# Stationary-weight units: order of high and low parts, and the columns at which their tiles start

## Chip, cores, metric

The kernel runs on one core of a Trainium2 chip. The metric is the device time of one execution in microseconds (us).

## What is computed

One decoder layer on 256 tokens of width 2048, in float32: a combined input projection, two token mixers (gated linear attention and forgetting attention), a merge and an output projection, a LayerNorm, a gated MLP of width 5632 with a causal convolution, a LayerNorm, and a gated embedding. Cut to the products that matter here:

```
proj = x @ w_in                        # gq, gk, gv, gr, glr, fq, fk, fv, ff, ma, mb
...
def conv_gated_mlp(x, w_gate, w_up, conv_w, conv_b, w_down):
    g = causal_dwconv(x @ w_gate, conv_w, conv_b)
    h = jax.nn.gelu(g) * (x @ w_up)
    return h @ w_down
```

The columns fq, fk (1024 each), gq, gk (1024 each) and the two matrices w_gate and w_up (5632 columns each) are the ones whose products the change touches.

## The kernel before

TensorE multiplies in the type float32r, which keeps fewer bits than float32. So each float32 operand is kept as two tiles, a high part (the value rounded to float32r) and a low part (what is left), and a product is three: high by high, high by low, low by high.

All weights come as units of 128 x 2048 floats, numbered 0 to 283 in the order of their use. `prep` loads a unit on SP's queue in two halves of 1024 columns (`raw`), makes the high part of each half on ScalarE (`hi`, by `copy`) and the low part on VectorE (`lo`, raw minus high). The tiles `hi` come from the pool `rhi`, the tiles `lo` from `rlo`, six buffers each. `unit()` hands out the next unit and prepares up to three ahead. TensorE and the other compute engines run in the order that a scheduler writes at build time; SP's queue runs in program order.

There are two ways to use a unit on TensorE:

- Stationary weights (`w_unit`): a unit holds 16 blocks of 128 rows by 128 output columns. For each block the high part is the stationary operand and the activation tile (x high and x low side by side, 512 columns) moves past it; then the low part is stationary and x high (256 columns) moves past. All 32 matmuls add into one bank of PSUM. This is done for fq and fk (units 0 to 15, `psfq`, `psfk`, with activations `xT`), for gq and gk (16 to 31, `psq`, `psk`) and for w_gate and w_up in turn (136 to 223, even numbers `psg`, odd `psu`, with activations `x1T`). The first three units of the last group go token half by token half through `w_phase` instead, with 256 columns in each matmul; so `w_unit` serves 117 units.
- Stationary activations (`q_unit`, `s_half`, `x_half`; lines 979, 841 and 353): the activation is stationary and 512 columns of `hi` or `lo` move. All other units go this way.

Small matmuls of other work are pulled in between: `tick(7)` in `w_unit` pulls one step of the attention after the eighth low matmul of a unit.

The tiles lie in SBUF one behind the other, and a pool's buffers lie at steps of the tile's width. Counted in float32 columns, `xT` and `x1T` start at a multiple of 64, and so do the buffers of `rhi` (1024 wide) and of `rlo` (1152 wide). `lo_tile` takes 1024 of the 1152 columns, from column 16 on in the stationary-weight units and from column 0 on in all others (`UA`, `LO_SHIFT`). "Place" below means a tile's first column within a period of 64. Some other tiles happen to lie at place 48: the stationary activation sums `xS` of two pairs (line 841), and the values `vh`, `vl` that move at line 1084.

Of the kernel before, what the change touches and what calls it, by code (L numbers as in the profile page):

```python
# [10 lines left out]
F32R = mybir.dt.float32r  # L11
# [8 lines left out]
P = 128  # L20
# [15 lines left out]
GAPS = (96, 64, 80)  # L36


LO_SHIFT = 16
UA = (range(32, 136), range(224, 284))  # L40
P_STAT = 5000
P_LN1 = (4000, 2000)
P_LN2 = (4000, 1000)
# [35 lines left out]
def tile_block(ctx: ExitStack, tc: tile.TileContext, wu, wfv, wpp, xT_in, x_in, pT_in, wlr,  # L79
               chan, gnorm, lng, ident_in, mask_in, cmask_in, out):  # L80
    nc = tc.nc
# [9 lines left out]
    rhi = ctx.enter_context(tc.tile_pool(name="rhi", bufs=6))  # L91
    rlo = ctx.enter_context(tc.tile_pool(name="rlo", bufs=6))
# [12 lines left out]
    def s8(shape, dt=F32, name=None):  # L105
        return big.tile(shape, dt, tag="S8", name=name)

    def t1(name):
        return sm.tile([P, 256], F32, tag="t1", bufs=6, name=name)
# [4 lines left out]
    def mmtile(name):  # L114
        return pmm.tile([P, 512], F32, tag="mm", name=name)
# [4 lines left out]
    def copy(o, i, scale=1.0):  # L120
        return nc.scalar.activation(o, i, AF.Copy, bias=0.0, scale=scale)  # L121
# [12 lines left out]
    n_prep, n_used = [0], [0]  # L134
# [15 lines left out]
    sd = dr.tile([len(DN_S[0]) // 2, P, 2048], F32, name="sd")  # L150
    hS = {}

    def lo_tile(u, name):
        o = 0 if any(u in r for r in UA) else LO_SHIFT
        return rlo.tile([P, 1152], F32R, tag="lo", name=f"lo{name}")[:, o:o + 1024]

    def differences(r0, r1, h, pinned=False):
        b12, b11, b22, b21 = r0[:, 0:512], r0[:, 512:1024], r1[:, 0:512], r1[:, 512:1024]
        sub = lambda o, a, b: nc.vector.tensor_tensor(o, a, b, ALU.subtract)  # L159
        if h == 0:  # L160
            i = sub(b11, b12, b11)
            if pinned:
                tc.keep_in_program_order(i)
            sub(b12, b12, b22)
        else:
            sub(b22, b22, b11)
            sub(b21, b21, b22)
# [17 lines left out]
    def prep_s(u):  # L185


        r0, r1 = [ring.tile([P, 1024], F32, tag="raw", bufs=5, name=f"raw{u}_{h}")
                  for h in range(2)]
        b12, b11, b22, b21 = r0[:, 0:512], r0[:, 512:1024], r1[:, 0:512], r1[:, 512:1024]  # L190
        rt = (r0, r1)
        if u in parked:
            nc.sync.dma_start(b11, wu[u, :, 512:1024])
            nc.sync.dma_start(r1, wu[u, :, 1024:2048])
            w = s8([P, 2048], name=f"td{u}")
            nc.sync.dma_start(w, td[parked[u]])
            rt = (w[:, 0:1024], w[:, 1024:2048])
        else:
            for h, r in enumerate((r0, r1)):
                nc.sync.dma_start(r, wu[u, :, h * 1024:(h + 1) * 1024])  # L200
        if dn0 <= u < dn0 + NF:
            nh = (u - dn0) // (NF // 2)
            pair = DN_ORDER[nh][(u - dn0) % (NF // 2)]
            i = DN_S[0].index(pair)
            if i % 2 == 0:
                two = s8([P, 8, 256], F32R, name=f"hS{nh}_{pair}")
                nc.sync.dma_start(two.bitcast(F32), sd[i // 2].rearrange(
                    "p (i n) -> p i n", i=8))
                hS[nh, pair], hS[nh, DN_S[0][i + 1]] = two[:, 0:4], two[:, 4:8]

        def split(src, name, e=slice(0, 1024)):
            hi = rhi.tile([P, 1024], F32R, tag="hi", name=f"hi{u}_{name}")[:, e]
            lo = lo_tile(u, f"{u}_{name}")[:, e]
            copy(hi, src)
            nc.vector.tensor_tensor(lo, src, hi.bitcast(F32), ALU.subtract)  # L215
            return [(hi[:, o:o + 512], lo[:, o:o + 512]) for o in range(0, src.shape[1], 512)]

        x11, = split(b11, "b11", slice(512, 1024))
        x22, x21 = split(r1, "b2")
        if u not in parked:  # L220
            differences(r0, r1, 0)
        t3, t1_ = split(rt[0], "t13")
        if u not in parked:
            differences(r0, r1, 1)
        t2_, t4 = split(rt[1], "t24")
        ready[u] = [x11, x21, x22, t1_, t3, t2_, t4]

    def prep(pinned=False):
        u = n_prep[0]
        n_prep[0] += 1  # L230
        if u in s_units:
            prep_s(u)
            return
        his, los = [], []
        for h in range(2):
            raw = ring.tile([P, 1024], F32, tag="raw", bufs=5, name=f"raw{u}_{h}")
            nc.sync.dma_start(raw, wu[u, :, h * 1024:(h + 1) * 1024])
            hi = rhi.tile([P, 1024], F32R, tag="hi", name=f"hi{u}_{h}")
            copy(hi, raw)
            lo = lo_tile(u, f"{u}_{h}")  # L240
            i = nc.vector.tensor_tensor(lo, raw, hi.bitcast(F32), ALU.subtract)  # L241
            if pinned:
                tc.keep_in_program_order(i)
            his.append(hi)
            los.append(lo)
        ready[u] = (his, los)


    def unit(ahead=3):
        u = n_used[0]  # L250
        n_used[0] += 1
        while n_prep[0] < min(NU, u + ahead):
            prep()
        return ready.pop(u)
# [42 lines left out]
            nc.gpsimd.tensor_copy(mask[:, 4 * i:4 * i + 4, :], maskf)  # L297


    def w_unit(ps, hi, lo, act, kts, first, last, hoff=0, tick=None):  # L300


        n = len(kts)
        for i, kt in enumerate(kts):
            a = act[kt // 4]
            w0 = (hoff + i) * P
            nc.tensor.matmul(ps, lhsT=hi[i // 8 if hoff == 0 else 0][:, w0 % 1024:w0 % 1024 + P],  # L307
                             rhs=a[:, kt % 4, :], start=first and i == 0, stop=False)
            nc.tensor.matmul(ps[:, 256:512],  # L309
                             lhsT=lo[i // 8 if hoff == 0 else 0][:, w0 % 1024:w0 % 1024 + P],  # L310
                             rhs=a[:, kt % 4, 0:256], start=False, stop=last and i == n - 1)
            if tick is not None:
                tick(i)

    def w_phase(ps, hi, lo, act, t, kts, part=slice(None)):

# [41 lines left out]
    def pull(n, gens=mixers):  # L358
        for _ in range(n):
            while gens:  # L360
                try:
                    next(gens[0])
                    break
                except StopIteration:
                    gens.pop(0)
# [92 lines left out]
    for u in range(8):  # L458
        hi, lo = fvu[u]
        for j in range(2):  # L460
            kt = 2 * u + j
            a = xT[kt // 4][:, kt % 4, :]
# [6 lines left out]
            for t, i, c in seq:  # L469
                o, n = fch[c]  # L470
                w, x = prods[t][i]
                nc.tensor.matmul(fbk[t][c][:, 0:n], lhsT=x, rhs=w[:, o:o + n],  # L472
                                 start=kt == 0 and i == 0, stop=kt == 15 and i == 2)
# [11 lines left out]
        elif u == 4:  # L485
            load_consts()
    prep()
    prep()
    wraw = s8([GROWS, 1024], name="wraw")
    nc.gpsimd.memset(wraw, 0.0)  # L490
# [15 lines left out]
    for t in range(2):  # L506
        for c, (o, n) in enumerate(fch):
            n = min(n, 1024 - o)
# [143 lines left out]
    for n in range(16):  # L652
        h, j = n // 2, n % 2
        hi, lo = unit()

        ps = (mxtile if n == 0 else mmtile)(f"psf{'qk'[j]}{h}")
        w_unit(ps, hi, lo, xT, range(16), True, True,
               tick=lambda i: pull(1) if i == 7 else None)
        if n % 8 == 0:
            fqk[h // 4] = s8([P, 4, 2, 256], name=f"fqk{h // 4}")  # L660
        comb(ps, fqk[h // 4][:, h % 4, j], (P ** -0.5, 1.0)[j])
        if n >= 1:
            pull(1, parks)
# [105 lines left out]
    for n in range(16):  # L769
        nm, dst, sc = (("q", gq, 1.0 / 16.0), ("k", gk, 1.0))[n // 2 % 2]  # L770
        h, c = n // 4, n % 2
        hi, lo = unit()
        ps = mmtile(f"ps{nm}{2 * h + c}")
        w_unit(ps, hi, lo, xT, range(16), True, True,
               tick=lambda i: pull(1, mixers if n < 4 else levels) if i == 7 else None)
        comb(ps, dst[:, h, :].rearrange("p (t c n) -> p t c n", t=2, c=2)[:, :, c, :], sc)
        if n >= 4:
            pull(1)
        if n >= 1:
            pull(1, parks)  # L780
# [346 lines left out]
    for n in range(PSM1, 32):  # L1127
        if n in (26, 28):
            i = n // 2 - 13
# [189 lines left out]
    pq, first = [], []  # L1319
# [92 lines left out]
    def gate_up(name):  # L1412
        if first:
            return first.pop(0)
        hi, lo = unit()
        ps = mmtile(name)
        w_unit(ps, hi, lo, x1T, range(16), True, True)
        return ps

    for n in range(NF):  # L1420
# [18 lines left out]
        u = t1("up")  # L1439
        comb(psu, u)  # L1440
        pair, j = n // 2, n % 2
        if n % 4 == 0:
            hC[n // 4] = (s8 if n < 40 else late.tile)([P, 4, 512], F32R, name=f"hC{n // 4}")
        if pair in DN_S[0]:
            if j == 0:
                yp = t2("yp").rearrange("p (k t) -> p k t", t=S)
            h = yp[:, j, :]
        else:
            h = y
# [4 lines left out]
        if pair in DN_S[0] and j == 1:  # L1454
            v = s_sums(yp)
            for i in range(2):
                w = sm.tile([P, 2, 256], F32R, tag="t2", bufs=6, name="hs")
# [4 lines left out]
                o = k % 2 * 1024 + 512 * i  # L1462
# [295 lines left out]
```

## Time and profile before

| what | value |
|---|---|
| median of three runs | 1645.18 us (1645.11 to 1647.18) |
| profiled execution, first to last instruction | 1645.0 us |
| TensorE matmuls (PE) | 8422, busy 1638.4 us |
| weight loads (PEld) | 8422, busy 1404.3 us |
| VectorE (DVE) | 1964 instructions, busy 1356.0 us |
| ScalarE (ACT) | 1277 instructions, busy 910.3 us |
| DMA traffic | 477.81 MB, mean 290 GB/s |

PE is a matmul and PEld the load of its stationary operand, which runs beside the matmul before it. Matmuls overlap in the trace (a row's duration goes beyond the next row's start), so what one costs is the distance between two starts. The span of the profiled execution, 1645.0 us, is all that is given of its time; it is 0.2 us under the median.

### The profile page before, as it was taken

Reading aid. Unit: us, or ns where it says so; the run is one execution under the profiler, and the core shown is the slowest. Engines: PE = TensorE matmul, PEld = TensorE weight load, DVE = VectorE, ACT = ScalarE, POOL = GpSimd, SP = SyncE. Lnnn points to the kernel's source line nnn. Section 1 sums busy time; section 2 is a strip of 40 time slices with the busy share of each in tenths; the row PEclk is TensorE's granted clock in tenths of the full one; section 3 lists DMA queues with packets and bytes.
Section 4 is the critical chain, followed back from the end, with each engine's and each line's share of the span. In section 5 each row is a group of like instructions: output and inputs, shape, how many; then the busy total and the mean of one; then the engine's idle time right before and its main releaser. Section 6 shows DMA issues by size and latency. Waiting matters only on the chain.

```text
span 1645.0 us, 23490 instructions
## 1 busy us (share of the span) xinstructions
PE 1638.4 (100%) x8422; PEld 1404.3 (85%) x8422; DVE 1356.0 (82%) x1964; ACT 910.3 (55%) x1277; POOL 92.7 (6%) x244
## 2 busy tenths in 40 slices
PE   9999999999999999999999999999999999999998
PEld 9988888888888888887898888888888888888887
DVE  7687899788989867778987888887887778988887
ACT  6655555456666654446574445555455456566554
POOL 0000000000000000000010111110111000000000
PEclk9999999999999999999999999999999999999999
DMA  8799799878888768889855898888766679899574
GB/s 324 281 371 341 290 383 356 294 258 309 306 333 307 252 207 303 305 335 364 296 190 194 315 338 320 308 306 304 279 239 217 210 260 336 305 343 348 177 258 157
DMA packets 114838, 477.81 MB, mean 290 GB/s; under 512 B 13032, under 2 KB 14320, under 8 KB 95136
## 3 DMA queue, kind: packets, MB, share of 16 engines
q1 hardware_dynamic: 105216, 417.57, 70.8%
q0 software_dynamic: 9504, 58.73, 8.9%
q8 instruction: 66, 1.08, 0.2%
q14 instruction: 52, 0.43, 0.1%
HBM read 417.53 MB, written 58.73 MB: 290 GB/s over the span
## 4 chain that ended last, share of the span: by engine, by line
PE 97%; DMA 1%; DVE 1%; ACT 0%; issue 0%; POOL 0%; ACTq 0%
PE psm L979 11%; PE dn L841 10%; PE psu L307 10%; PE psg L307 9%; PE psa L979 5%; PE psu L309 5%; PE psg L309 5%; PE dn_p L841 4%; PE gr L841 3%; PE gv L841 3%; PE fv L472 3%; PE pg L353 3%; PE psb L979 3%; PE wo L841 2%; PE gr_p L841 2%; PE gv_p L841 2%
## 5 line engine op out<-in xcount | busy, mean ns | idle before, releaser
L241 DVE TENSOR_TENSOR lo<-raw,hi 128x1024 fp32r<-128x1024 f32 x456 | 551.1, 1220 | 140.7 <-ACT hi L121 139.4
L121 ACT ACTIVATE hi<-raw 128x1024 fp32r<-128x1024 f32 x456 | 476.6, 1057 | 304.2 <-DMA raw<-in_wu_dram 83.7
L307 PE MATMUL psu<-x1T,hi 128*128 128x512 f32 x688 | 240.4, 392 | 0.0
L307 PE MATMUL psg<-x1T,hi 128*128 128x512 f32 x672 | 234.8, 392 | 0.0
L309 PE MATMUL psu<-x1T,lo 128*128 128x256 f32 x688 | 192.3, 280 | 0.0
L309 PE MATMUL psg<-x1T,lo 128*128 128x256 f32 x672 | 187.8, 280 | 0.0
L979 PE MATMUL psm<-hi,xT 128*128 128x512 f32 x512 | 163.0, 392 | 0.0
L307 PEld LDWEIGHTS psu<-x1T,hi 128*128 128x128 f32 x688 | 129.2, 188 | 27.6
L307 PEld LDWEIGHTS psg<-x1T,hi 128*128 128x128 f32 x672 | 126.2, 188 | 27.0
L309 PEld LDWEIGHTS psu<-x1T,lo 128*128 128x128 f32 x688 | 130.6, 190 | 0.0
L121 ACT ACTIVATE hi_b<-raw 128x512 fp32r<-128x512 f32 x112 | 92.9, 841 | 66.8 <-DMA raw<-in_wu_dram 17.9
L309 PEld LDWEIGHTS psg<-x1T,lo 128*128 128x128 f32 x672 | 127.6, 190 | 0.0
L159 DVE TENSOR_TENSOR td<-td 128x512 f32<-128x512 f32 x172 | 117.6, 684 | 0.9
L215 DVE TENSOR_TENSOR lo_b<-raw,hi_b 128x512 fp32r<-128x512 f32 x112 | 104.9, 952 | 15.9 <-ACT hi_b L121 15.6
L979 PEld LDWEIGHTS psm<-hi,xT 128*128 128x128 f32 x512 | 96.2, 188 | 19.6
L215 DVE TENSOR_TENSOR lo_t<-td,hi_t 128x1024 fp32r<-128x1024 f32 x86 | 101.7, 1219 | 12.7 <-ACT hi_t L121 12.0
L121 ACT ACTIVATE hi_t<-td 128x1024 fp32r<-128x1024 f32 x86 | 88.0, 1053 | 28.9 <-DMA td<-td 15.1
L979 PE MATMUL psm<-lo,xT 128*128 128x512 f32 x256 | 99.8, 390 | 0.0
L841 PE MATMUL dn<-hi,hC 128*128 128x512 f32 x352 | 97.8, 389 | 0.0
L979 PE MATMUL psa<-hi,oT 128*128 128x512 f32 x256 | 81.2, 392 | 0.0
L841 PEld LDWEIGHTS dn<-hi,hC 128*128 128x128 f32 x352 | 66.0, 188 | 13.7
L979 PEld LDWEIGHTS psa<-hi,oT 128*128 128x128 f32 x256 | 48.1, 188 | 10.0
(414 smaller groups left out, 3130.8 us busy)
## 6 DMA issues: line engine op xcount, KB each, us to landing
raw<-in_wu_dram SPq DMA_DIRECT2D x525, 512.0 KB, 6.3
td<-in_wu_dram SPq DMA_DIRECT2D x43, 1024.0 KB, 8.8
td<-td POOLq DMA_DIRECT2D x43, 1024.0 KB, 7.7
td<-td SPq DMA_DIRECT2D x43, 1024.0 KB, 8.3
hS<-sd SPq DMA_DIRECT2D x11, 1024.0 KB, 8.8
raw<-in_wu_dram SPq DMA_DIRECT2D x43, 256.0 KB, 7.7
fvraw<-in_wfv_dram SPq DMA_DIRECT2D x13, 524.0 KB, 6.6
sd<-hs POOLq DMA_DIRECT2D x24, 256.0 KB, 5.6
```

Of the source, the lines that this page charges most:

```text
L121: return nc.scalar.activation(o, i, AF.Copy, bias=0.0, scale=scale)
L159: sub = lambda o, a, b: nc.vector.tensor_tensor(o, a, b, ALU.subtract)
L215: nc.vector.tensor_tensor(lo, src, hi.bitcast(F32), ALU.subtract)
L241: i = nc.vector.tensor_tensor(lo, raw, hi.bitcast(F32), ALU.subtract)
L307: nc.tensor.matmul(ps, lhsT=hi[i // 8 if hoff == 0 else 0][:, w0 % 1024:w0 % 1024 + P], rhs=a[:, kt % 4, :], start=first and i == 0, stop= ...
L309: nc.tensor.matmul(ps[:, 256:512], lhsT=lo[i // 8 if hoff == 0 else 0][:, w0 % 1024:w0 % 1024 + P], rhs=a[:, kt % 4, 0:256], start=False, ...
L353: nc.tensor.matmul(bs[j][:, 0:m], lhsT=x, rhs=v[:, o:o + m], start=first and i == 0, stop=last and i == 2)
L472: nc.tensor.matmul(fbk[t][c][:, 0:n], lhsT=x, rhs=w[:, o:o + n], start=kt == 0 and i == 0, stop=kt == 15 and i == 2)
L841: nc.tensor.matmul(ps[:, e], lhsT=x, rhs=w, start=k == 1, stop=k == total.get(id(ps), 3 * ns))
L979: nc.tensor.matmul(ps[t], lhsT=x, rhs=v, start=first and i == 0 and j == 0, stop=last and i == 3 and j == 2)
```

## The change

The units of the stationary-weight way (0 to 31 and 136 to 223) are counted in a list `UW`. Those at an even position keep the order high, low, high, low, and those at an odd position multiply eight high blocks, then the eight low blocks of the same half, then the same for the second half. With the order of `UW`, odd are the units of fk, every second unit of gq and gk, and all of w_up except the first, which goes through `w_phase`: 59 units in blocks of eight, 58 alternating.

The places change for all these units. An alternating unit takes a pair (place of high, place of low) from the list `SH`, in turn; a unit in blocks has its high part at 0 and its low part at 0, 4, 8 and so on to 60, in turn. All other units have both at 0, as before. Both tiles are now 1088 columns wide (17 times 64), so that every second buffer starts at 64 within 128. Six buffers of 1088 and six of 1088 are as long as six of 1024 and six of 1152, so that the tiles behind the two pools stay where they were.

```
+UW = [*range(32), *range(136, 224)]
+SH = ((16, 4), (16, 60), (24, 60), (20, 0), (20, 4), (20, 60), (20, 56), (24, 0), (24, 4),
+      (22, 60), (16, 2), (18, 2), (18, 4), (18, 0), (18, 62))
...
+    def place(u):
+        if u not in UW:
+            return 0, 0
+        w = UW.index(u)
+        return (0, w // 2 % 16 * 4) if w % 2 else SH[w // 2 % len(SH)]
+
     def lo_tile(u, name):
-        o = 0 if any(u in r for r in UA) else LO_SHIFT
-        return rlo.tile([P, 1152], F32R, tag="lo", name=f"lo{name}")[:, o:o + 1024]
+        o = place(u)[1]
+        return rlo.tile([P, 1088], F32R, tag="lo", name=f"lo{name}")[:, o:o + 1024]
+
+    def hi_tile(u, name):
+        o = place(u)[0]
+        return rhi.tile([P, 1088], F32R, tag="hi", name=f"hi{name}")[:, o:o + 1024]
...
-            hi = rhi.tile([P, 1024], F32R, tag="hi", name=f"hi{u}_{h}")
+            hi = hi_tile(u, f"{u}_{h}")
...
         n = len(kts)
-        for i, kt in enumerate(kts):
-            a = act[kt // 4]
-            w0 = (hoff + i) * P
-            nc.tensor.matmul(ps, lhsT=hi[i // 8 if hoff == 0 else 0][:, w0 % 1024:w0 % 1024 + P],
-                             rhs=a[:, kt % 4, :], start=first and i == 0, stop=False)
...
+        m = 8 if UW.index(n_used[0] - 1) % 2 else 1
+
+        def high(i, kt):
+            w0 = i * P
+            nc.tensor.matmul(ps, lhsT=hi[i // 8][:, w0 % 1024:w0 % 1024 + P],
+                             rhs=act[kt // 4][:, kt % 4, :], start=first and i == 0, stop=False)
+
+        def low(i, kt):
...
+        steps = list(enumerate(kts))
+        for j in range(0, n, m):
+            for i, kt in steps[j:j + m]:
+                high(i, kt)
+            for i, kt in steps[j:j + m]:
+                low(i, kt)
+                if tick is not None:
+                    tick(i)
```

How the order on PE moves, at two places. First unit 1, the first of fk, around the middle of the unit, where a pulled step (`psg` of `gS`) stands. `xT_112` and the like are the activation tiles, `hi_0`, `lo_0` the first half's parts, `hi_1`, `lo_1` the second's. Before:

```order
L307 MATMUL psfk_751<-xT_113,hi_0_600 128x512
L309 MATMUL psfk_751<-xT_113,lo_0_602 128x256
L554 MATMUL psg_768<-gSt,wS 128x256 x2
L307 MATMUL psfk_751<-xT_114,hi_1_606 128x512
L309 MATMUL psfk_751<-xT_114,lo_1_608 128x256
```

And after:

```order
L319 MATMUL psfk_751<-xT_112,hi_0_600 128x512 x4
L319 MATMUL psfk_751<-xT_113,hi_0_600 128x512 x4
L324 MATMUL psfk_751<-xT_112,lo_0_602 128x256 x4
L324 MATMUL psfk_751<-xT_113,lo_0_602 128x256 x4
L576 MATMUL psg_768<-gSt,wS 128x256 x2
L319 MATMUL psfk_751<-xT_114,hi_1_606 128x512 x4
L319 MATMUL psfk_751<-xT_115,hi_1_606 128x512 x4
```

The eight high matmuls of a half now stand together ahead of its eight low ones; the pulled step stays between the halves.

Second the gate and up stage, PE, unit 139 (`psu_8057`), where the second half of its blocks begins. Before:

```order
L307 MATMUL psu_8057<-x1T_7632,hi_0_7828 128x512
L309 MATMUL psu_8057<-x1T_7632,lo_0_7830 128x256
L307 MATMUL psu_8057<-x1T_7633,hi_1_7834 128x512
L309 MATMUL psu_8057<-x1T_7633,lo_1_7836 128x256
L307 MATMUL psu_8057<-x1T_7633,hi_1_7834 128x512
```

And after, to the start of the gate unit behind it (`psg_8109`):

```order
L319 MATMUL psu_8057<-x1T_7633,hi_1_7834 128x512 x4
L319 MATMUL psu_8057<-x1T_7634,hi_1_7834 128x512 x4
L324 MATMUL psu_8057<-x1T_7633,lo_1_7836 128x256 x4
L324 MATMUL psu_8057<-x1T_7634,lo_1_7836 128x256 x4
L319 MATMUL psg_8109<-x1T_7631,hi_0_7860 128x512
L324 MATMUL psg_8109<-x1T_7631,lo_0_7862 128x256
```

The up unit has its highs in a run and its lows in a run; the gate unit behind it still alternates.

More of the change, by code (lines that the diff above doesn't have):

```diff
@@ L36 @@
 GAPS = (96, 64, 80)
-LO_SHIFT = 16
-UA = (range(32, 136), range(224, 284))
+UW = [*range(32), *range(136, 224)]
+SH = ((16, 4), (16, 60), (24, 60), (20, 0), (20, 4), (20, 60), (20, 56), (24, 0), (24, 4),
+      (22, 60), (16, 2), (18, 2), (18, 4), (18, 0), (18, 62))
 P_STAT = 5000
@@ L211, in split @@
         def split(src, name, e=slice(0, 1024)):
-            hi = rhi.tile([P, 1024], F32R, tag="hi", name=f"hi{u}_{name}")[:, e]
+            hi = hi_tile(u, f"{u}_{name}")[:, e]
             lo = lo_tile(u, f"{u}_{name}")[:, e]
@@ L297, in load_consts2, with w_unit @@
             nc.gpsimd.tensor_copy(mask[:, 4 * i:4 * i + 4, :], maskf)
-    def w_unit(ps, hi, lo, act, kts, first, last, hoff=0, tick=None):
+    def w_unit(ps, hi, lo, act, kts, first, last, tick=None):
         n = len(kts)
-        for i, kt in enumerate(kts):
-            a = act[kt // 4]
-            w0 = (hoff + i) * P
-            nc.tensor.matmul(ps, lhsT=hi[i // 8 if hoff == 0 else 0][:, w0 % 1024:w0 % 1024 + P],
-                             rhs=a[:, kt % 4, :], start=first and i == 0, stop=False)
[L309 to L313, printed above, removed]
+        m = 8 if UW.index(n_used[0] - 1) % 2 else 1
[4 more added lines that the diff above has]
+        def low(i, kt):
+            w0 = i * P
+            nc.tensor.matmul(ps[:, 256:512], lhsT=lo[i // 8][:, w0 % 1024:w0 % 1024 + P],
+                             rhs=act[kt // 4][:, kt % 4, 0:256], start=False,
+                             stop=last and i == n - 1)
+        steps = list(enumerate(kts))
[6 more added lines that the diff above has]
+                    tick(i)
     def w_phase(ps, hi, lo, act, t, kts, part=slice(None)):
```

## The prediction

> **What bounds the kernel now.** First the busy times, the granted clock and TensorE's waits.
>
> ```profile
> PE 1638.4 (100%) x8422; PEld 1404.3 (85%) x8422; DVE 1356.0 (82%) x1964; ACT 910.3 (55%) x1277; POOL 92.7 (6%) x244
> PEclk9999999999999999999999999999999999999999
> PE warm_ps L131 <- DVE warm L128: 1.2, 1, 1.2
> PE wo L841 <- DVE lo_b L215: 0.4, 1, 0.4
> PE wo_p L841 <- ACT hi_t L121: 0.2, 1, 0.2
> ```
>
> TensorE works from end to end at the full granted clock, and all its waits for others come to 1.8 us. The time is therefore a sum over matmuls, and only what a matmul costs can move it. So next: the groups of the stationary-weight units, and then single starts. I use the distance from one start to the next (a step), since the durations overlap.
>
> ```profile
> L307 PE MATMUL psu<-x1T,hi 128*128 128x512 f32 x688 | 240.4, 392 | 0.0
> L307 PE MATMUL psg<-x1T,hi 128*128 128x512 f32 x672 | 234.8, 392 | 0.0
> L307 PE MATMUL psfq<-xT,hi 128*128 128x512 f32 x128 | 46.4, 402 | 0.0
> ```
>
> With psfk, psq and psk (128 each, like psfq) that is 1872 high matmuls of 512 columns in 117 units of 16, each with a low matmul of 256 columns behind it.
>
> ```profile
> 855.02 0.39 PE L307 MATMUL psg<-x1T,hi 128*128 128x512 f32 x1
> 855.25 0.28 PE L309 MATMUL psg<-x1T,lo 128*128 128x256 f32 x1
> 855.37 0.39 PE L307 MATMUL psg<-x1T,hi 128*128 128x512 f32 x1
> ...
> 1315.39 0.39 PE L307 MATMUL psu<-x1T,hi 128*128 128x512 f32 x1
> ...
> 855.02 0.19 PEld L309 LDWEIGHTS psg<-x1T,lo 128*128 128x128 f32 x1
> 855.25 0.19 PEld L307 LDWEIGHTS psg<-x1T,hi 128*128 128x128 f32 x1
> ```
>
> From unit 140's first matmul (855.02) to unit 223's (1315.39) lie 83 whole units with nothing between: 460.37 us / 1328 pairs = 346.7 ns a pair. The load rows start with the matmul before theirs: the low part's 128 columns are read while the high matmul streams, and the other way round. That is where the places of two tiles can meet.
>
> **What a matmul costs by kind and place.** By place I mean a tile's first column within a period of 64 columns. In the program as built x, x1 and the high parts lie at place 0 and the low parts of these units at 16. Elsewhere other pairs of places occur, so the same trace has prices.
>
> ```profile
> 1415.67 22.44 PE dn L841 x99
> ...
> 1635.98 0.40 PE L909 MATMUL pg_11b<-hi,x2T 128*128 128x256 f32 x2
> ...
> 1637.78 0.28 PE L909 MATMUL pg_11b<-hi,x2T 128*128 128x256 f32 x1
> ...
> 837.64 0.28 PE L322 MATMUL psg<-x1T,hi 128*128 128x256 f32 x1
> ...
> 842.14 0.28 PE L322 MATMUL psg<-x1T,hi 128*128 128x256 f32 x1
> ...
> 395.45 0.39 PE L841 MATMUL gv<-hi_b,xS 128*128 128x512 f32 x1
> ...
> 398.20 0.39 PE L841 MATMUL gv<-hi_t,xT 128*128 128x512 f32 x1
> ...
> 542.67 0.39 PE L1084 MATMUL go<-vh,ath 128*128 128x512 f32 x1
> ...
> 544.07 0.39 PE L1084 MATMUL go<-vh,ath 128*128 128x512 f32 x1
> 544.31 0.39 PE L1084 MATMUL go<-vl,ath 128*128 128x512 f32 x1
> 544.53 0.39 PE L1084 MATMUL go<-vh,atl 128*128 128x512 f32 x1
> ```
>
> Both operands at place 0, a new stationary tile for each matmul: 512 columns take 22.44/99 = 226.7 ns; 256 columns take (1637.78 - 1635.98)/15 = 120.0 ns. The 256 columns between them cost 106.7 ns, so each matmul carries 13.3 ns beside its stream. The two steps add to 346.7, the pair of today: there, too, each matmul carries 13.3 ns on average.
>
> Row A, line 322 with line 326, 256 columns, stationary tiles at 0 and 16 in turn: 4.50/38 = 118.4 ns, 1.6 less. Row B, stationary tile xS at place 48 (12 matmuls): 2.75/12 = 229.2, 2.5 more. Row C, moving tile at 48, stationary at 0 (6 matmuls): 1.40/6 = 233.3, 6.6 more; right behind them one whose moving tile lies at 0 takes 0.22 again. So places do change a step, by a few ns in either direction.
>
> **The change part by part.** No instruction comes or goes on PE, and SP's queue issues the same DMAs in the same order. On PE only the order inside 59 of the 117 units differs; on ScalarE and VectorE some small rows of other work have changed places with a neighbour, which costs nothing while TensorE waits 1.8 us in all.
>
> *Blocks of eight alone.* 8 x 226.7 + 8 x 120.0 = 8 x 346.7 where both parts lie at 0. A run of highs and a run of lows are the two rows measured singly above. I take 0.
>
> *Places in the 59 blocked units (944 pairs).* The high parts stay at 0: their term is 0. The lows run over 16 places, 0 to 60 in steps of 4. Rows at hand: place 0 gives 0, A (16) -1.6, B (48) +2.5; mean +0.3 ns, 944 x 0.3 = +0.3 us. C is a moving tile displaced, so I keep it as an end: 944 x -1.6 = -1.5 us to 944 x 6.6 = +6.2 us.
>
> *Places in the 58 alternating units (928 pairs).* The high parts go to 16 to 24, the lows to between 56 and 4. Behind a high's 512 columns now a tile near place 0 is loaded, as at line 841: no change. Behind a low's 256 columns one from 16 to 24 is loaded; nearest is A, -1.6. Whether the high step gains as well no row says; I give it half of A, -0.8. Together -2.4 ns, 928 x -2.4 = -2.2 us. Ends: A for both, -3.2 ns or -3.0 us; B for the high and C for the low, +9.1 ns or +8.4 us.
>
> *The tiles' width.* Both pools now have buffers of 1088 columns (17 x 64) for 1024 and 1152, so every second buffer starts at 64 of 128; together they are as large as before, and all tiles behind them keep their addresses. In other stages these buffers are the moving operand (some 3700 matmuls of 512 columns), still at place 0. The one kind of 512 columns that has both operands at 64 of 128 today is pp:
>
> ```profile
> 1545.38 1.53 PE L353 MATMUL pp<-pw,pTs 128*128 128x512 f32 x6
> ```
>
> (1.53 - 0.39)/5 = 228 ns, within the rounding of two decimals of 226.7. I take 0; at 1 ns each it would be 3.7 us either way.
>
> *ScalarE and VectorE* write the parts to places that are no multiple of 16 columns. In the gate and up stage:
>
> ```profile
> 855.00:1315.00 460.00, 460.00 (x2656) 406.75 (x2655) 368.46 (x597) 234.35 (x358) 53.64 (x165) 1.00 0.76 275
> L241 DVE TENSOR_TENSOR lo<-raw,hi 128x1024 fp32r<-128x1024 f32 x456 | 551.1, 1220 | 140.7 <-ACT hi L121 139.4
> ```
>
> VectorE, the third pair of numbers, is busy for 368.46 of 460 us. Its 166 low parts there (83 units, two each, 1.22 us: 203 us) could grow by 91.5/203 = 45% before it filled the stage; TensorE's cover is gone only then. Cost 0.
>
> *Buffers.* A blocked unit wants its first low tile after eight highs, 8 x 226.7 = 1.8 us instead of 0.2 into the unit, and frees its first high tile 0.9 us sooner. With 1.8 us of waits in all there is nothing to gain, and nobody is made later. A pulled step of attention still stands behind the eighth low matmul. Cost 0.
>
> Sum: 0.3 - 2.2 = -1.9 us on the profiled span of 1645.0 us, 0.2 us under the median of 1645.18. Against that median: 1643.3 us. A measurement of this kernel tells about 0.2% (3.3 us) from no change, so this is no change.
>
> **A rule against the rows.** The Trainium skill, "TensorE: Matmul & The Clock Gate", Step-by-step, says that the moving operand and the weight load have independent read ports in SBUF, so that loading the next tile takes nothing from the running matmul. By that rule no place has a price and the time stays at 1645.2. Rows B and C disagree, by 2.5 and 6.6 ns a matmul, so I give the rule only the small chance below.
>
> **The rivals.**
>
> *Nothing changes.* As a mechanism here: the load's stalls always fit into the 13.3 ns, wherever the tiles lie. For it: blocks and pairs add to the same 346.7 ns, and A, B and C are rows of 38, 12 and 6 steps. Against: C holds in every one of its six steps. It gives 1645.2.
>
> *The places save more.* In every step with a displaced tile the 13.3 ns become A's 11.7, or less. -3.2 x 928 and -1.6 x 944 make -3.0 - 1.5 = -4.5 us, 1640.7. For it: the places are many, and A's is the only price for 256 columns. Against: no settled row lies lower than A. If some places saved twice as much, -9.0 us, 1636.2: the low end.
>
> *Slower: the steps do not settle.* After transposes the matmuls take some ten steps until they are regular.
>
> ```profile
> 1557.79 0.60 PE L1223 MATMUL ptl<-ident,z 128*128 128x128 f32 x4
> 1558.14 0.72 PE L353 MATMUL pg<-hi,x2T 128*128 128x512 f32 x2
> 1558.70 0.63 PE L353 MATMUL pg<-lo,x2T 128*128 128x512 f32 x2
> 1559.16 1.09 PE L353 MATMUL pg<-hi,x2T 128*128 128x512 f32 x4
> 1560.09 0.62 PE L353 MATMUL pg<-lo,x2T 128*128 128x512 f32 x2
> 1560.55 1.07 PE L353 MATMUL pg<-hi,x2T 128*128 128x512 f32 x4
> 1561.46 0.62 PE L353 MATMUL pg<-lo,x2T 128*128 128x512 f32 x2
> 1561.91 0.39 PE L353 MATMUL pg<-hi,x2T 128*128 128x512 f32 x1
> ```
>
> From 1558.70 to 1560.55 eight steps take 231.3 ns each, 4.6 above 226.7; from 1560.55 to 1561.91 six take 226.7. The regular step is thus a state that is found, and today's pairs are in it. Blocks that switch every eight matmuls, with lows at odd places, may never find it: 944 x 4.6 = +4.3 us, and in the alternating units, if 16 to 24 does not fit, 928 x 4.6 = +4.3 us: 1653.8. It decides from some 720 unsettled highs of 1872 on (720 x 4.6 = 3.3 us). Against it: with both parts at place 0 a run of lows is as regular as a run of highs.
>
> **How the numbers follow.** The sum as worked out, with its own range of 1641.5 to 1648.5: 0.42 (0.31 within 0.2%, 0.08 faster, 0.03 slower). Nothing changes: 0.10. The places save more: 0.26, counted as faster. The steps do not settle: 0.22 (0.02 of it within). That makes faster 0.34, same 0.43, slower 0.23. For 8 in 10 the range goes to 1636.5 below, near twice A, and to 1652 above, where the alternating units pay about 7 ns a pair or most highs are unsettled.
>
> **What the profile after would show.** Step by step: a blocked unit lasts 16 x 346.7 = 5547 ns, its run of eight highs 8 x 226.7 = 1.81 us, its run of eight lows 0.95 to 0.98; an alternating unit lasts 5508 (16 x 344.3). Lines 841 and 979 keep 226.7, TensorE's waits stay under 2 us, VectorE's low parts at 1220 ns. I am wrong if gate and up units differ from 5547 by more than 100 ns (1.8% of a unit, 117 units: 11 us), if one half does it alone, or if steps at line 841 have moved, which the buffers' width would have to explain.

## The result, and the profile after

| kernel | median | lowest to highest | runs |
|---|---|---|---|
| before | 1645.14 us | 1644.41 to 1647.18 | 18 |
| after | 1647.99 us | 1647.62 to 1649.02 | 18 |

The ratio is 1.0018 (95% interval 1.0010 to 1.0025): 2.85 us longer. That lies in the forecast range and just inside the 0.2% that the prediction took for no change. But the interval is clear of 1, and the sign is not the forecast's: 1643.3 us was predicted.

First the page of the kernel after: busy times, granted clock, TensorE's one wait, and the chain of work that ended last.

```profile
PE 1640.1 (100%) x8422; PEld 1403.0 (85%) x8422; DVE 1357.6 (82%) x1964; ACT 910.0 (55%) x1277; POOL 92.3 (6%) x244
PEclk9999999999999999999999999999999999999999
PE 99%; DVE 0%; ACT 0%; POOL 0%; issue 0%; ACTq 0%
L252 DVE TENSOR_TENSOR lo<-raw,hi 128x1024 fp32r<-128x1024 f32 x456 | 551.3, 1220 | 138.8 <-ACT hi L122 137.6
PE warm_ps L132 <- DVE warm L129: 1.2, 1, 1.2
```

TensorE is still the bound, at the same clock, with less waiting than before (1.2 us), and VectorE's low parts still take 1220 ns at their new places. So the time went into the matmuls themselves. To see which, take the two stages of stationary weights, each from its first regular start to the first start of the stage behind it. Timelines, in each row start, duration, line and operation; first the kernel before (its first row, 855.02, is in the prediction).

```profile
51.40 0.48 PE L307 MATMUL psfq<-xT,hi 128*128 128x512 f32 x1
...
248.22 0.40 PE L979 MATMUL psm<-hi,xT 128*128 128x512 f32 x1
...
1320.94 0.63 PE L841 MATMUL dn<-hi,hC 128*128 128x512 f32 x2
```

The same places of the kernel after:

```profile
51.06 0.48 PE L319 MATMUL psfq<-xT,hi 128*128 128x512 f32 x1
...
248.43 0.39 PE L1001 MATMUL psm<-hi,xT 128*128 128x512 f32 x1
...
853.77 0.39 PE L319 MATMUL psg<-x1T,hi 128*128 128x512 f32 x1
...
1321.94 0.62 PE L863 MATMUL dn<-hi,hC 128*128 128x512 f32 x2
```

Units 0 to 31 took 196.82 us before and take 197.37 now: +0.55. Units 140 to 223 (84 units, 1344 pairs) took 1320.94 - 855.02 = 465.92 us, 346.67 ns a pair, and take 468.17, 348.34 a pair: +2.25. Together +2.8 us, the whole of the measured difference.

The spans of the two profiles differ by less, 1646.0 against 1645.0, because the profiled execution of before was not one of its quicker ones: it lost some 1.5 us in the output projection, around the two waits at line 841 that the prediction shows (0.4 and 0.2 us). No later profile has them. An execution whose own time is known stands 1.7 us above its span (widths_only below: 1644.83 us, span 1643.1), so before's profiled execution took about 1646.7. Against widths_only the kernel after is 2.9 us longer in span.

Now into the units. Unit 165 in blocks, then the alternating units 166 (high part at place 16, low at 60) and 210 (24 and 4), kernel after:

```profile
993.29 2.01 PE L319 MATMUL psu<-x1T,hi 128*128 128x512 f32 x8
995.14 1.10 PE L324 MATMUL psu<-x1T,lo 128*128 128x256 f32 x8
996.07 2.01 PE L319 MATMUL psu<-x1T,hi 128*128 128x512 f32 x8
...
998.85 0.39 PE L319 MATMUL psg<-x1T,hi 128*128 128x512 f32 x1
...
1004.29 0.40 PE L319 MATMUL psu<-x1T,hi 128*128 128x512 f32 x1
...
1243.68 0.40 PE L319 MATMUL psg<-x1T,hi 128*128 128x512 f32 x1
...
1249.35 0.63 PE L319 MATMUL psu<-x1T,hi 128*128 128x512 f32 x2
```

The run of eight highs takes 1.85 us, where 1.81 was forecast, and the eight lows 0.93. The whole blocked unit takes 5.56, unit 166 5.44, unit 210 5.67; 5.55 was the length of each of these before. Over the 84 units from 140 on, worked out from every start of those lines:

| units | mean pair | high step | low step |
|---|---|---|---|
| before | 346.67 ns | 229.6 | 117.1 |
| after, 42 in blocks | 348.57 | 230.3 | 118.3 |
| after, 42 alternating | 348.11 | 231.4 | 116.7 |

Both halves of the change became dearer, by 1.9 and 1.4 ns a pair. For the blocks the position in a run tells how. Mean step of the first to the eighth high over the 86 runs in units 139 to 223 of the kernel after, in ns: 232.8, 233.1, 229.8, 230.1, 229.5, 228.7, 227.3, 231.2; of the lows: 117.2, 118.6, 118.4, 119.2, 118.2, 118.4, 117.7, 118.4. A run of highs comes down to about 227 only at its seventh step, and the eighth, beside which the first low tile is loaded, is dearer again.

For the alternating units no such rule is to be read off. In the gate units each pair of places of the list `SH` comes up two or three times. Ten of the fifteen pairs keep their price within 1.5 ns, (16, 60) for instance with 340.0 and 341.0 ns a pair. The other five do not: (20, 60) takes 355.4, 348.3 and 347.7, (18, 4) takes 353.3, 347.2 and 346.8. And unit 2, in the stage of fq and fk, takes some 351 at (16, 60) if its pulled step is left out. So places matter, but the same two places can have different prices.

### The profile page after: what moved, and what is told of

It is laid out like the page before. It is cut to its first block, busy times and chain, and to the rows that moved or that the text cites. A ratio compares the mean times of both kernels' runs of the same rounds, so it can differ in the third digit from the quotient of the medians.

```text
span 1646.0 us, 23492 instructions
## 1 busy us (share of the span) xinstructions
PE 1640.1 (100%) x8422; PEld 1403.0 (85%) x8422; DVE 1357.6 (82%) x1964; ACT 910.0 (55%) x1277; POOL 92.3 (6%) x244
## 4 chain that ended last, share of the span: by engine, by line
PE 99%; DVE 0%; ACT 0%; POOL 0%; issue 0%; ACTq 0%
PE psm L1001 11%; PE dn L863 10%; PE psu L319 10%; PE psg L319 9%; PE psa L1001 5%; PE psu L324 5%; PE psg L324 5%; PE dn_p L863 4%; PE wo L863 3%; PE gr L863 3%; PE gv L863 3%; PE fv L494 3%; PE pg L375 3%; PE psb L1001 3%; PE gr_p L863 2%; PE gv_p L863 2%
## 5 line engine op out<-in xcount | busy, mean ns | idle before, releaser
L252 DVE TENSOR_TENSOR lo<-raw,hi 128x1024 fp32r<-128x1024 f32 x456 | 551.3, 1220 | 138.8 <-ACT hi L122 137.6
L319 PE MATMUL psu<-x1T,hi 128*128 128x512 f32 x688 | 172.4, 392 | 0.0
L319 PEld LDWEIGHTS psu<-x1T,hi 128*128 128x128 f32 x688 | 123.2, 188 | 23.9
L170 DVE TENSOR_TENSOR td<-td 128x512 f32<-128x512 f32 x172 | 117.7, 685 | 1.1
L324 PEld LDWEIGHTS psu<-x1T,lo 128*128 128x128 f32 x688 | 93.4, 188 | 7.1
L324 PE MATMUL psu<-x1T,lo 128*128 128x256 f32 x688 | 95.4, 281 | 0.0
```

The lines of the kernel that those rows point to most:

```text
L319: nc.tensor.matmul(ps, lhsT=hi[i // 8][:, w0 % 1024:w0 % 1024 + P], rhs=act[kt // 4][:, kt % 4, :], start=first and i == 0, stop=False)
L324: nc.tensor.matmul(ps[:, 256:512], lhsT=lo[i // 8][:, w0 % 1024:w0 % 1024 + P], rhs=act[kt // 4][:, kt % 4, 0:256], start=False, stop=last ...
```

## The experiments

Times below are medians; each ratio is against runs of the kernel before on the same chip (medians 1645.45, 1645.40 and 1645.60 us in the three groups). "Pair" is a high and a low step together, and a stage's pair is its 84 units from 140 on, as above. By "pattern" I mean a sequence of steps that repeats.

### The order and the length of the blocks, all tiles at place 0

**alt_0_0**: the kernel before, alternating, with its low parts moved from 16 to 0.

```
-LO_SHIFT = 16
+LO_SHIFT = 0
```

> The kernel before, with the low tiles of the stationary-weight units at place 0 instead of 16; the order high, low, high, low stays. In the changed kernel the units in blocks with both parts at 0 took 349.3 ns a pair against 346.7 before. Theory 1 (after each change of kind TensorE needs some seven matmuls to find its regular step, so a switch every eight matmuls costs, and the place 0 does not): the alternating order finds its regular step here too, 226.7 + 120.0 = 346.7 ns a pair, 1645.2 us. Theory 2 (the places cost, the order does not): 349.3 ns in 1872 pairs, 2.6 x 1872 = +4.9 us, 1650.0 us.

Measured: 1655.44 us (1654.97 to 1656.01), ratio 1.0060 (1.0047 to 1.0073). Timeline, first in units 0 to 31, then in the gate and up stage:

```profile
119.37 0.40 PE L307 MATMUL psfk<-xT,hi 128*128 128x512 f32 x1
...
123.61 0.40 PE L307 MATMUL psfk<-xT,hi 128*128 128x512 f32 x1
...
145.69 0.39 PE L307 MATMUL psfk<-xT,hi 128*128 128x512 f32 x1
...
152.62 0.39 PE L307 MATMUL psq<-xT,hi 128*128 128x512 f32 x1
...
854.74 0.40 PE L307 MATMUL psg<-x1T,hi 128*128 128x512 f32 x1
...
1329.62 0.40 PE L841 MATMUL dn<-hi,hC 128*128 128x512 f32 x1
```

From 119.37 to 123.61 lie 12 pairs: 353.3 ns each. From 145.69 to 152.62 lie 20: 346.5. The gate stage's 1344 pairs take 474.88 us: 353.3, every unit alike (highs 241, 236, 232 and lows 120, 113, 118, repeating every three pairs). So at the same places, in the same execution, two patterns exist, and a whole stage stays in one of them. No theory had this. The sum of two steps measured singly, 226.7 + 120.0 = 346.7, doesn't give the price of a pair.

**blk4_0_0, blk8_0_0, blk16_0_0**: both parts at place 0, all 117 units in blocks of 4, 8 or 16 (`w_unit` as in the change).

```
-LO_SHIFT = 16
+LO_SHIFT = 0
...
+        m = 8            # 4 and 16 in the other two
```

> All 117 stationary-weight units in blocks of eight, both parts at place 0, tiles as wide as before. Theory 1 and theory 2 both say 349.3 ns a pair as in three units of the changed kernel: +4.9 us, 1650.0. If the three units were a chance of what stood ahead of them, 346.7 and 1645.2. Together with the alternating kernel at the same places it gives the price of the order alone: +4.9 us by theory 1, 0 by theory 2.

> The same with blocks of sixteen: all highs of a unit, then all its lows. Theory 1: the first eight highs take 229.6 on average, the next eight 226.7, the lows 118.3 and then 120.0: 228.2 + 119.2 = 347.4 ns a pair, +1.3 us, 1646.5. Theory 2 (places): 349.3 ns as in blocks of eight, 1650.0.

> All 117 stationary-weight units in blocks of four, both parts at place 0, tiles as wide as before. Theory 1 (each run of highs pays the same start-up: 233, 236, 228, 233, 231, 227, 227, 226 ns in the trace with blocks of eight, the lows 113, 119 and then 120): a run of four has the mean of the first four, 232.5 + 118.0 = 350.5 ns a pair against 349.1 with eight and 348.0 with sixteen, and 346.7 before: 3.8 x 1872 = +7.1 us, 1652.5. Rival (a fixed price of the order, whatever the length of the run): 349.1 as with eight, 1650.0.

| blocks of | median | ratio (95%) | pair |
|---|---|---|---|
| 4 | 1652.72 us | 1.0046 (1.0034 to 1.0059) | 350.8 ns |
| 8 | 1649.96 us | 1.0027 (1.0016 to 1.0037) | 349.2 |
| 16 | 1647.76 us | 1.0014 (1.0006 to 1.0023) | 347.9 |

One unit of each, blocks of 4 (16 pairs from row to row):

```profile
969.92 1.09 PE L308 MATMUL psg<-x1T,hi 128*128 128x512 f32 x4
970.85 0.63 PE L313 MATMUL psg<-x1T,lo 128*128 128x256 f32 x4
...
975.53 0.63 PE L308 MATMUL psu<-x1T,hi 128*128 128x512 f32 x2
```

Blocks of 8:

```profile
966.27 2.00 PE L308 MATMUL psg<-x1T,hi 128*128 128x512 f32 x8
968.11 1.11 PE L313 MATMUL psg<-x1T,lo 128*128 128x256 f32 x8
...
971.85 2.00 PE L308 MATMUL psu<-x1T,hi 128*128 128x512 f32 x8
```

Blocks of 16:

```profile
966.34 3.82 PE L308 MATMUL psg<-x1T,hi 128*128 128x512 f32 x16
970.00 2.08 PE L313 MATMUL psg<-x1T,lo 128*128 128x256 f32 x16
971.91 3.82 PE L308 MATMUL psu<-x1T,hi 128*128 128x512 f32 x16
```

Units of 5.61, 5.58 and 5.57 us. Within a run of 16 the highs take 233, 236, 228, 233, 231 and from the sixth on 226.7; the lows 119.5 on average. A run of eight begins with the same five steps and ends settled. Shorter blocks pay the beginning more often: this is the rival "the steps do not settle", as a start-up of five steps, and blk4_0_0 came out where that expects it and not at a fixed price per pair. In runs of eight the highs cost 3.4 ns more than settled ones on average (230.1), and the lows give 0.9 back (119.1 against 120.0), which is why eight cost 2.5 ns a pair and not the rival's 4.6. Set against alt_0_0, though, blocks of eight are 5.5 us shorter: whether blocks cost or gain depends on the pattern in which the alternating order would have run.

### The parts of the change, one at a time

**widths_only**: the change without blocks (`m = 1`) and with the places of before, so that only the 1088 columns are left.

```
-        return (0, w // 2 % 16 * 4) if w % 2 else SH[w // 2 % len(SH)]
+        return 0, 16
...
-        m = 8 if UW.index(n_used[0] - 1) % 2 else 1
+        m = 1
```

> The changed kernel with places 0 and 16 in all stationary-weight units and no blocks: of the change only the tile widths of 1088 remain, with every second buffer at 64 of 128. Theory 1 (a regular state that the alternating order keeps; the period of places is 64): 346.7 ns a pair and 226.7 ns at the stages with stationary activations as before, 1645.2. Rival: the 64 of 128 matters, in these stages (1 ns a matmul is 3.7 us) or by another state of the pairs (353.1 ns: +12 us).

```profile
51.11 0.48 PE L319 MATMUL psfq<-xT,hi 128*128 128x512 f32 x1
...
247.93 0.40 PE L1001 MATMUL psm<-hi,xT 128*128 128x512 f32 x1
...
853.10 0.39 PE L319 MATMUL psg<-x1T,hi 128*128 128x512 f32 x1
...
1319.02 0.63 PE L863 MATMUL dn<-hi,hC 128*128 128x512 f32 x2
```

1645.12 us, ratio 0.9998 (0.9989 to 1.0007). Both stages take to the hundredth what they took before, 196.82 and 465.92 us, and the steps of the other stages are 226.8 (line 863) and 227.3 (line 1001), as before. The widths cost nothing.

**blocks_only**: the kernel before, its places and widths too, with every odd unit in blocks of eight.

```
+        m = 8 if UW.index(n_used[0] - 1) % 2 else 1
```

> The kernel before with its widths and its places 0 and 16, and every second unit in blocks of eight. Theory 1 (a block costs its seven settling steps whatever the places; the alternating pairs behind it fall back into the one state that 0 and 16 showed): blocked units at 347.1 ns a pair as those with low place 16 in the changed kernel, alternating ones at 346.7 plus a few ns in their first pairs: +0.4 to +1.0 us, 1645.6 to 1646.2. Rival (the state of the alternating units is drawn anew behind each block): some of them at 340 or 353, up to 6 us either way, 1639 to 1651.

1647.58 us, ratio 1.0012 (1.0003 to 1.0021). An alternating unit (160) and a blocked one (161), first rows, and the first of the unit behind them:

```profile
965.08 0.40 PE L309 MATMUL psg<-x1T,hi 128*128 128x512 f32 x1
...
970.64 0.40 PE L309 MATMUL psu<-x1T,hi 128*128 128x512 f32 x1
...
976.21 0.40 PE L309 MATMUL psg<-x1T,hi 128*128 128x512 f32 x1
```

Over the stage the blocked units take 348.44 ns a pair and the alternating ones between them 347.40: their first pairs pay (236 + 121 in the first), then they are back at 346.7. Blocks alone thus cost 2.2 us, 1.8 ns a blocked pair and 0.7 in each pair that follows. The direction was expected, the size was not (347.1 was expected for the blocked ones, and 1645.6 to 1646.2 us).

**after_no_blocks**: the change with its places, but all units alternating (`m = 1`).

> The changed kernel with all its places, but every unit alternates. Theory 1 (state kept, blocks cost): the 59 units fall from 348.5 to about 346.7 ns a pair, -1.7 us against the changed kernel, 1646.3. Rival (places set the state in alternating units): units with the high at 0 and the low near 0 run at 353 as in the kernel with all places at 0, and carry this state on: 59 x 16 x 4.5 ns = +4.2 us, 1652.

1647.81 us, ratio 1.0017 (1.0008 to 1.0026). Stage:

```profile
853.88 0.40 PE L319 MATMUL psg<-x1T,hi 128*128 128x512 f32 x1
...
1321.65 0.63 PE L863 MATMUL dn<-hi,hC 128*128 128x512 f32 x2
```

467.77 us, 348.04 ns a pair, with single units anywhere from 340.0 to 355.9. Neither 1646.3 nor 1652 was met: the odd units take 348.5 ns a pair now that they alternate, as they did in blocks. The places alone cost 2.4 us, the blocks alone 2.2, both together 2.85. The parts don't add: what a unit costs depends on what stood ahead of it.

### One pair of places everywhere

**alt_16_60**: the change's widths, all units alternating, every high part at 16 and every low part at 60, a pair of places at which the kernel after had shown 340.0 (unit 166) and some 351 (unit 2).

```
-        return (0, w // 2 % 16 * 4) if w % 2 else SH[w // 2 % len(SH)]
+        return 16, 60
...
+        m = 1
```

> The changed kernel with no blocks: all 117 units alternate, all with the high part at 16 and the low part at 60. In the changed kernel two of three units with this pair of places ran at 340.0 and 341.0 ns a pair (steps of 227 and 113), one at 350.8. Theory 1 (a regular state that is found and then kept while nothing changes): it is kept from unit to unit, 6.4 ns x 1872 = -12.0 us, 1633.2 us. Rival: the state depends on what stands ahead and on the buffer (starts at 0 or 64 of 128), so half of the units stay at 347: -6 us, 1639; or units find it only by chance, 1645.

Its twelve runs, all at a granted clock of 0.999 or 1.0, fall into two groups, three from 1635.46 to 1638.58 us and nine from 1653.86 to 1654.33, so the median, 1654.03, and the ratio, 1.0025 (0.9999 to 1.0051), describe neither. The profiled execution is the 1635.46 one:

```profile
81.28 0.40 PE L319 MATMUL psfk<-xT,hi 128*128 128x512 f32 x1
...
86.93 0.40 PE L319 MATMUL psfq<-xT,hi 128*128 128x512 f32 x1
...
852.39 0.39 PE L319 MATMUL psg<-x1T,hi 128*128 128x512 f32 x1
...
1309.64 0.63 PE L863 MATMUL dn<-hi,hC 128*128 128x512 f32 x2
```

Unit 5 takes 5.65 us, 353.3 ns a pair (235 + 118); the gate and up stage 457.25 us, 340.2 a pair (227 + 113). Again two patterns at the same places in one execution. If the other nine runs had their 85 gate and up units at 353.3, they would be 85 x 16 x 13.3 ns = 18.1 us longer; they are 18.4 to 18.9 longer than the fastest. None of them was profiled, so that is worked out, not shown.

**seeded_16_60**: if a pattern is found at the entry and then kept, a block in front could make the entry always the same. Units 0 to 138 as before (0 and 16); in the gate and up stage all at (16, 60) and alternating, but every twelfth unit a "seed" in blocks of eight at (0, 52).

```
+SEED = range(139, 224, 12)
...
+        if u < 139:
+            return 0, 16
+        return (0, 52) if u in SEED else (16, 60)
...
+        m = 8 if n_used[0] - 1 in SEED else 1
```

> High at 16 and low at 60 in the alternating units of the gate and up stage from unit 139 on, where the kernel with these places everywhere ran at 340.0 ns a pair, and in its long runs must have stayed in another state (235 + 118 = 353, as in its units 5 to 7). Units 139, 151, 163 and so on to 223 (8 of 85) are in blocks of eight with places 0 and 52, which sets the state anew; units 0 to 138 as before at 0 and 16. Theory 1 (the state is found behind a block, and kept): 77 units at 340.0 ns, 8 at 346.3: 77 x 16 x -6.7 = -8.3 us, 1636.9, in every run. Rival (the state is a matter of chance also behind a block): runs between 1637 and 1654, a median over 1645.

1637.09 us (1636.86 to 1639.52), ratio 0.9951 (0.9939 to 0.9964). Stage:

```profile
853.34 0.40 PE L321 MATMUL psg<-x1T,hi 128*128 128x512 f32 x1
...
1310.16 1.09 PE L326 MATMUL psu<-x1T,lo 128*128 128x256 f32 x8
```

The last row is the last run of lows of unit 223, itself a seed; the stage ends at 1311.10, 457.76 us, 8.16 less than before. Seeds take 346.1 ns a pair, the unit behind a seed 341.0, the others 340.0. The expectation held: no run of the five is near 1654, and the highest, 1639.52, is 2.6 us above 1636.9. This version beats both kernels.

**two_seeds**: the same with seeds at 139 and 181 alone.

```
+SEED = (139, 181)
```

> The kernel with places 16 and 60 in the gate and up stage, but only units 139 and 181 in blocks, not every twelfth. Theory 1 (a state, once found, is kept while nothing but pairs follows): six units fall from 346.1 to 340.0 ns a pair and the six behind them from 341.0: 6 x 16 x 7 = 0.7 us better than with eight such units, 1636.4, in every run. Rival (the state is lost now and then, and the frequent blocks brought it back): some runs up to 9 us longer.

1636.98 us (1636.39 to 1637.85), ratio 0.9947 (0.9934 to 0.9961). The pattern is kept over 41 units, even across a wait of 0.76 us at unit 156 (wait in brackets):

```profile
940.52 0.44 PE L321 MATMUL psg<-x1T,hi 128*128 128x512 f32 x1
941.72 0.40 PE L326 MATMUL psg<-x1T,lo 128*128 128x256 f32 x1 [0.76 <-DVE lo L254]
...
947.09 0.39 PE L321 MATMUL psu<-x1T,hi 128*128 128x512 f32 x1
...
952.53 0.39 PE L321 MATMUL psg<-x1T,hi 128*128 128x512 f32 x1
```

Unit 156 takes 6.57 us, 1.1 more than at 340.0 ns a pair, and unit 157 is back at 5.44 us, 340.0 a pair. The profiled execution took 1637.46 us; two of the five, 1636.39 and 1636.44, took the expected 1636.4. Fewer seeds gain nothing that this measurement can tell (the two intervals overlap).

**seeds_everywhere**: seeds in units 0 to 31 as well, every odd one.

```
+SEED = (*range(1, 32, 2), 139, 181)
...
+        if 136 <= u < 139:
+            return 0, 16
```

> The same, and in units 0 to 31 every second unit in blocks of eight with places 0 and 52, the others alternating at 16 and 60. Theory 1: behind a block the alternating units begin at 340 ns a pair, until the step pulled into their middle throws them into 340, 347 or 353 for the second half: 16 x 16 x (343.5 - 347.3) = -1.0 us and the blocked ones 16 x 16 x (346.3 - 346.8) = -0.1 us, 1635.3. Rival (the pulled steps leave them mostly at 353): 16 x 8 x 6.4 = +0.8 us over half of each unit, no gain or a loss, 1636.4 to 1637.

1638.64 us (1635.51 to 1640.97), ratio 0.9954 (0.9941 to 0.9966); 1635.3 was expected, and two of the five runs, 1635.51 and 1635.90, lie near it. Units 0 to 31 did become 1.5 us shorter (195.33 against 196.82). But see, behind the two rows that bound these units, the gate and up stage at unit 156 in the profiled execution, the one of 1638.96 us:

```profile
51.43 0.48 PE L321 MATMUL psfq<-xT,hi 128*128 128x512 f32 x1
...
246.76 0.40 PE L1003 MATMUL psm<-hi,xT 128*128 128x512 f32 x1
...
939.34 0.50 PE L321 MATMUL psg<-x1T,hi 128*128 128x512 f32 x1 [0.17 <-ACT hi L123]
940.60 0.39 PE L326 MATMUL psg<-x1T,lo 128*128 128x256 f32 x1 [0.76 <-DVE lo L254]
...
946.02 0.39 PE L321 MATMUL psu<-x1T,hi 128*128 128x512 f32 x1
...
951.57 0.39 PE L321 MATMUL psg<-x1T,hi 128*128 128x512 f32 x1
```

TensorE came to tiles that weren't ready, 0.93 us of waiting. Behind it unit 157 (946.02 to 951.57) takes 5.55 us, 346.7 a pair, and so do the units up to 180, until the seed at 181: 24 units x 16 x 6.7 ns = 2.6 us. The waits cost less than the pattern that was lost with them: units 155 and 156 together take 1.6 us more than two units at 340.0. But the wait of 0.76 us alone stands in two_seeds too, and there the pattern came back. So a wait can lose it and need not; what decides is not shown.

## Why the prediction was right or wrong

*What bounds the kernel: right.* TensorE without waits, full clock, and all of the difference in the steps of the changed units.

*Blocks of eight alone, taken as 0: wrong, the first failing step.* The two rows were read from long, settled runs (99 and 15 steps), and a run of eight is mostly start-up. Measured with both parts at 0: 349.2 against 346.7, +2.5 ns. The prediction had the start-up in hand, as its third rival, and argued it away with "a run of lows is as regular as a run of highs"; once settled it is, but not in its first steps.

*Places in the blocked units, +0.3 ns: about right.* 348.6 in the change against 349.2 with all at 0 is -0.6 ns, inside the ends. So the blocked units cost 944 x 1.9 = +1.8 us in all (the stage's price for every blocked pair) against a forecast of +0.3.

*Places in the alternating units, -2.4 ns: wrong, the second failing step.* The low step moved by -0.4 (117.1 to 116.7) instead of -1.6, the high by +1.8 instead of -0.8: +1.4 ns a pair, 928 x 1.4 = +1.3 us against a forecast of -2.2. The size isn't the point. The step assumed that each place has a price and that a pair's price is the sum; alt_0_0 (353.3 and 346.5 at the same places) and alt_16_60 (340.2 and 353.3) show that it has several. The -1.6 and +2.5 ns of rows A and B may each have been one draw of this kind; that is argued, not shown. (The two terms make +3.1 us where +2.85 was measured, because units 0 to 31 rose by less than their share.)

*Widths, VectorE, ScalarE, buffers, the pulled step, all 0: right.* widths_only shows the first, 1220 ns at line 252 the second, TensorE's waits of 1.2 us the rest.

*The rivals.* "Nothing changes", 1645.2, came nearest in time, but its mechanism (the 13.3 ns hold every stall, wherever the tiles lie) falls with alt_0_0: +10 us from one shift of 16 columns. The rule that the prediction weighed, the Trainium skill's "TensorE: Matmul & The Clock Gate", Step-by-step, by which loading the next tile takes nothing from the running matmul, does not agree with the same run, where a place did have a price; that the load is what costs the time is not isolated. "The places save more" exists, but only where the pattern of 340 is entered and kept: 8.3 us, about twice its price. "The steps do not settle" has the right sign and, for the blocks, the right mechanism, at a third of its price (+2.85 of +8.6 us).

*Its own tests.* The run of eight highs was 1.85 us, not 1.81; the lows 0.93 to 0.95, at the lower edge; alternating units 348.11 x 16 = 5570 ns, not 5508. The steps at lines 863 and 1001 stayed.

*What stays open.* Why such patterns exist was not isolated: what in reading two tiles meets, and when, or whether other engines' use of the same memory has a part. Nor was which one is entered after a given neighbour; the seed's places came from what the kernel after had shown, not from a rule. That the seed makes the entry sure rests on 15 runs of three kernels, none over 1641.0 us, against 3 good runs of 12 without it. Those 12 ran on another chip, with (16, 60) in units 0 to 31 too, and a kernel that differs by the seed alone was not run; nor was it told apart whether the seed's order or its places do it.

## What to carry to other kernels

Where TensorE is never idle, measure a sequence as it will run: the price of a step in a long run of its kind is not its price in a run of eight, and two steps measured singly needn't add. Where the same instructions show two prices in one trace, look at what stood ahead of them, and repeat the run: a gain that hangs on an entry has to be made sure (here by a block of another order in front; a place where TensorE waits can undo it, as one of two waits did here). And after such a gain check the supply, since a quicker engine can meet waits that the slower one did not (here in the gate and up stage of two of the four quicker profiles, and of none of the others).

## What the runs showed of the hardware

- Back-to-back matmuls with a new stationary tile each (512 and 256 columns in turn) run in one of several repeating patterns, about 340.0, 346.7 or 353.3 ns a pair at a full granted clock, some 4% from end to end, and can keep it over 40 units and more (two_seeds: 141 to 180, all but unit 156 at 340.0).
- After a change from 256 to 512 columns, with all tiles at place 0, a run of matmuls takes five steps (233, 236, 228, 233, 231 ns) until it settles at 226.7 (blk16_0_0).
- Waits of 0.93 us in all were followed by 24 units in a dearer pattern, 2.6 us (seeds_everywhere): more was lost behind them than in them. After a wait of 0.76 us at the same place in two_seeds the pattern of 340.0 came back.
- Where tiles start in SBUF decides which patterns turn up: 16 columns' shift of the low parts alone moved the kernel by 10.0 us (1645.45 to 1655.44).
